# Logits from 64-row matmuls, two sets to a pair of PSUM banks, in a four-layer decoder kernel

## The chip, the core and the metric

The kernel runs on one core of a Trainium2 chip. Five engines work side by side: PE (TensorE, matmuls, with PEld for its weight loads), DVE (VectorE), ACT (ScalarE), POOL (GpSimd) and SP, which issues the DMAs. Each engine takes its own instructions in order and waits on semaphores for the others. The metric is the device time of one execution in microseconds (us), the median of three runs; a trace of one more execution shows every instruction with its start and its duration.

## What is computed

A decoder trunk of four layers over 256 positions, width 1024, all in fp32. A layer projects x to queries, keys and values, mixes tokens, adds attention into 256 memory tokens, projects back, normalises, and runs a SwiGLU feed-forward net (FFN). Layers 0 and 3 use the first of three token mixers, layer 1 the second, layer 2 the third; every mixer has 12 heads of width 64, and the memory attention has 4.

```python
for i in range(DEPTH):
    kind, j = i % N_MIXERS, i // N_MIXERS
    if kind == 0:   # indexer scores choose 64 keys per query, then attention over these
        dots = jnp.einsum('bqhd,bsd->bqhs', qi, k_idx)
        score = jnp.einsum('bqhs,bqh->bqs', jax.nn.relu(dots), wi)   # 8 heads of width 64
        ...
        logits = jnp.einsum('bqhd,bqkhd->bhqk', qb, ks) * scale
        p = jax.nn.softmax(logits, axis=-1)
        ...
    mixed = jnp.concatenate([mix, mo], -1) @ w_out[i]     # mo: memory attention
    x = layer_norm(ALPHA * x + mixed, ln1_g[i], ln1_b[i])
    x = layer_norm(ALPHA * x + swiglu(x, w_gate_up[i], w_down[i]), ln2_g[i], ln2_b[i])
```

## The kernel before

Positions are taken in two blocks of 128 (`tb` 0 and 1). To come near fp32 accuracy, every operand is split into a high part, rounded to fp32r, and a low part, the rest: the high part is a cast on ACT, the low part a subtraction on DVE (`split`, L260), and a product is three matmuls, high by high, high by low and low by high (`mm3`, L253). Weights come in pieces by DMA, ACT casts them (L214), and DVE (L230) or POOL (L228) takes the difference. Projections are L256 to L258.

The order of the work on PE is written out by the program: `K` runs the pieces of a plan one after the other, and between pieces it calls `tick`, which moves a list of small tasks (generators) one step on. A task gives a `yield n` to wait n ticks; so rope, transposes, logits, softmax and the product with the values of a head pair lie between the projection pieces of later ones. On the other engines a scheduler sets the order from priorities.

PSUM has eight banks of 512 fp32 columns. Before, these are eight tiles in a list (`Slots`), taken from the front and put back at the end. A task that finds none free waits a tick.

A *set* of logits belongs to one pair of heads and one `tb`: 128 queries against `nk` = 128 keys (`tb` 0) or 256 (`tb` 1, and the memory attention), for both heads, in one bank. The head width is 64, half the rows of the array. The kernel before fills all 128 rows by stacking: the query tile `q` of a head holds its high part in its own 64 rows and its low part in the other 64 (`q_parts`, L479, one cast and one difference of 64 rows for each head), and the key tile holds the high part of the head in both halves, the low part beside it. For this ACT copies the keys' parts across the halves (`k_cross`, L490, two copies, L492 and L493). One product of 256 keys is then two matmuls for each head (L504, four in a set), one of 128 keys is one for each head, with the high and the low keys side by side (L500, two in a set). There are 80 sets: 24 for the heads and the memory attention in layer 0 and as many in layer 3, counting 8 of the indexer in each, and 16 each in layers 1 and 2.

After a set, `exps` (L515) takes the least of each row on DVE (with a mask L524 and L526, without one L521) and ACT takes the exponential of one head at a time with the row's sum (L529, an ACTIVATE and a READ_ACCUMULATOR each), in place. Three ticks later DVE multiplies by the reciprocal of the sum into `E` or `e` (L542), and the bank goes back. In layers 0 and 3 the indexer's sets are read by a copy and a relu on ACT (L717, L719) and summed on DVE (L728, L730).

Of the kernel before, what the change touches and what calls it, by code (L numbers as in the profile page):

```python
# [84 lines left out]

class Slots:
# [26 lines left out]
class K:  # L113
    def __init__(self, tc, io, ctx):
# [11 lines left out]
        self.banks = Slots([self.pp.tile([128, 512], F32, name=f"bank{i}") for i in range(8)])  # L126
# [10 lines left out]
        self.kks = one([128, 2, 2, S], "k", NKB, F32R)  # L137
# [3 lines left out]
        self.mk = [T([128, 2, 2, S], F32R, f"mk{i}") for i in range(2)]  # L141
# [337 lines left out]
    def q_parts(self, dst, src, scale=None):  # L479

        lo, hi = slice(0, 64), slice(64, 128)
        return [(dst[lo, 0], dst[hi, 0], src[lo], scale), (dst[hi, 1], dst[lo, 1], src[hi], scale)]

    def k_parts(self, dst, src):

        d = dst.rearrange("p h a t -> p a h t")
        n = src.shape[1]
        return d[:, 0], d[:, 1], src[:, None, :].to_broadcast([128, 2, n]), None

    def k_cross(self, dst):  # L490
        lo, hi = slice(0, 64), slice(64, 128)
        self.nc.scalar.copy(dst[hi, 0], dst[lo, 0])  # L492
        self.nc.scalar.copy(dst[lo, 1], dst[hi, 1])  # L493

    def logits(self, b, q, ks, nk):

        mm = self.nc.tensor.matmul
        for h in range(2):
            if nk == 128:
                mm(b[:, h * 256:h * 256 + 256].rearrange("p (a s) -> p a s", a=2), lhsT=q[:, h], rhs=ks[h][:, :, 0:128],  # L500
                   start=True, stop=True)
            else:
                for part in range(2):
                    mm(b[:, h * 256:h * 256 + 256], lhsT=q[:, h], rhs=ks[h][:, part], start=part == 0, stop=part == 1)  # L504

    def pair_logits(self, b, q, kb, nk):
        self.logits(b, q, [kb[:, h] for h in range(2)], nk)

    def read_logits(self, b, nk):
        if nk == 128:  # L510
            L = b.rearrange("p (h a s) -> p h a s", h=2, a=2)
            return L[:, :, 0], L[:, :, 1]
        return (b.rearrange("p (h s) -> p h s", h=2),)
# [17 lines left out]
    def softmax(self, nk, product, mask=None):  # L531

        nc = self.nc
        b = yield from self.tk(self.banks)
        st = yield from self.tk(self.sts)
        e = yield from self.tk(self.es[nk])
        product(b)
        L = self.read_logits(b, nk)
        self.exps(L, e, st[:, 0:2], st[:, 2:4], mask)
        yield W_EXP  # L540
        nc.vector.reciprocal(st[:, 4:6], st[:, 2:4])
        nc.vector.tensor_tensor(e, L[0], st[:, 4:6, None].to_broadcast([128, 2, nk]), op=OP.mult)  # L542
        self.banks.put(b)
        self.sts.put(st)
        yield W_NORM
        return e
# [35 lines left out]
    def qk_task(self, bank, tb, kb, q, flags):  # L582
        b, p = yield from self.rotated(bank, tb)
        q[tb] = yield from self.tk(self.qs)
        k = kb[:, :, :, tb * 128:tb * 128 + 128]
        self.split(self.k_parts(k, p[:, 1]), *self.q_parts(q[tb], p[:, 0], SCALE))
        self.k_cross(k)
        self.banks.put(b)
        yield W_K
        flags.add(("k", tb))  # L590

    def head_task(self, bank, tb, kb, q, flags, masks, vs, vi, col, mix, kbi):
        yield from self.qk_task(bank, tb, kb, q, flags)
        while not (("k", 0) in flags and masks[tb] is not None):
            yield 1
        nk = 128 * (tb + 1)

        def product(b):
            self.pair_logits(b, q[tb], kb, nk)
# [25 lines left out]
    def mk_piece(self, l):  # L625
        b, p = self.t_mode(self.memT, ("mk", l, 0))
        self.split(*(self.k_parts(self.mk[pp], p[:, pp]) for pp in range(2)))
        for pp in range(2):
            self.k_cross(self.mk[pp])
# [10 lines left out]
    def qm_piece(self, l):  # L640
        b, p = self.t_mode(self.xT, ("qm", l, 0))
        qm = [self.take(self.qms, "qm") for _ in range(2)]
        self.split(*(x for pp in range(2) for x in self.q_parts(qm[pp], p[:, pp], SCALE)))
# [4 lines left out]
    def mem_task(self, qm, pp, tb, mix):  # L648
        ts = slice(tb * 128, tb * 128 + 128)

        def product(b):
            self.pair_logits(b, qm[pp][:, :, ts], self.mk[pp], S)
# [12 lines left out]
    def ki_task(self, bank, tb, kb, wi, kg, kbb, flags):  # L665
# [21 lines left out]
        self.split((kb[:, 0, 0, tb * 128:tb * 128 + 128], kb[:, 0, 1, tb * 128:tb * 128 + 128], b[:, 0:128], None))  # L687
# [4 lines left out]
    def qi_task(self, bank, tb, c, qi, mix):  # L692
# [3 lines left out]
        self.split(*(x for i in range(2) for x in self.q_parts(qi[tb, 2 * c + i], p[:, i])))  # L696
# [4 lines left out]
    def select_task(self, tb, qi, kb, wi, flags, masks):  # L701
# [6 lines left out]
        for pr in range(4):  # L708
            while (tb, "ready", pr // 2) not in qi:
                yield 1  # L710
            b = yield from self.tk(self.banks)
            rl = yield from self.tk(self.es[nk])
            self.logits(b, qi[tb, pr], [kb[:, 0]] * 2, nk)
# [151 lines left out]
    def dil_task(self, bank, tb, kb, q, flags, g, parts, jp):  # L865
# [8 lines left out]
        b = yield from self.tk(self.banks)  # L874
        e = yield from self.tk(self.es[nk])
        self.pair_logits(b, q[tb], kb, nk)
# [324 lines left out]
```

## Time and profile before

| | |
|---|---|
| median of 3 runs | 1350.88 us (1350.25 to 1352.53) |
| the profiled execution | 1351.82 us, of which the span of its instructions 1350.0 us |
| mean granted TensorE clock | 0.983 of full speed |
| PE busy | 1287.3 us (95%) |
| DVE / ACT / POOL busy | 897.5 (66%) / 762.9 (57%) / 316.4 us (23%) |

Busy is the union of an engine's instructions in time, so PE's matmuls, which overlap each other, count once. A mean over the span mixes two kinds of stretches: four FFNs with the projections around them, and four mixers. Times within the trace are counted from the start of the span.

### The profile page before, as it was taken

To read this page: it belongs to the slowest core of one execution; us is meant where nothing else is said; L and a number is where in the kernel's file an instruction comes from. 1 tells how busy PE (TensorE), PEld (TensorE's weight loads), DVE (VectorE), ACT (ScalarE), POOL (GpSimd) and SP (SyncE) were. 2 spreads that over 40 slices of the span, in tenths; PEclk is the share of its full clock that TensorE was granted. 3 is DMA by queue.
4 is the path that set the end of the run, shared out by engine and by line. 5 is a ranking of instruction groups with operands and counts; after the bars stand their busy time and mean duration, and the time that the engine had idled before them with its cause. 6 is when DMAs were issued, how large, how long until landed. Compare 5 with 4: busy or idle time off the path is not lost. (4 is left out here: it accounts for less than half of the span.)

```text
span 1350.0 us, 24249 instructions
## 1 busy us (share of the span) xinstructions
PE 1287.3 (95%) x9186; PEld 1212.5 (90%) x9186; DVE 897.5 (66%) x1940; ACT 762.9 (57%) x1512; POOL 316.4 (23%) x277
## 2 busy tenths in 40 slices
PE   6889899999999789999999999999999899999997
PEld 5879799999999779999989989999999898899996
DVE  7887775555578886555567877555568997655555
ACT  5668754444469745444447986444445897544441
POOL 3434440000045343000034444000014533300000
PEclk9989999999999889999999999999999999999999
DMA  8443356556564136565545345666546333655551
GB/s 300 126 149 110 110 180 199 187 188 184 170 203 150 70 103 240 185 189 180 183 155 180 133 141 169 206 185 188 186 138 218 127 125 126 203 188 188 187 176 59
DMA packets 63190, 225.65 MB, mean 167 GB/s; under 512 B 7776, under 2 KB 7776, under 8 KB 63072
## 3 DMA queue, kind: packets, MB, share of 16 engines
q1 hardware_dynamic: 62784, 224.10, 50.2%
q8 instruction: 72, 1.18, 0.4%
q14 instruction: 46, 0.38, 0.1%
q10 hardware_dynamic: 288, 0.00, 0.0%
HBM read 223.02 MB, written 1.05 MB: 166 GB/s over the span
## 5 line engine op out<-in xcount | busy, mean ns | idle before, releaser
L214 ACT CAST wh<-raw 128x1024 fp32r<-128x1024 f32 (+1 forms) x402 | 420.8, 1048 | 318.6 <-PE bank L257 177.2
L230 DVE TENSOR_TENSOR wl<-raw,wh 128x1024 fp32r<-128x1024 f32 (+1 forms) x294 | 378.2, 1288 | 273.9 <-ACT wh L214 269.1
L228 POOL TENSOR_TENSOR wl<-raw,wh 128x512 fp32r<-128x512 f32 x216 | 296.7, 1399 | 727.7 <-ACT wh L214 718.2
L256 PE MATMUL bank<-xh,wh 128*128 128x256 f32 x1344 | 382.1, 284 | 0.0
L257 PE MATMUL bank<-xl,wh 128*128 128x256 f32 x1344 | 381.2, 284 | 0.0
L258 PE MATMUL bank<-xh,wl 128*128 128x256 f32 x1344 | 381.2, 284 | 0.0
L257 PEld LDWEIGHTS bank<-xl,wh 128*128 128x128 f32 x1344 | 258.6, 192 | 1.2
L256 PEld LDWEIGHTS bank<-xh,wh 128*128 128x128 f32 x1344 | 258.6, 192 | 1.3
L258 PEld LDWEIGHTS bank<-xh,wl 128*128 128x128 f32 x1344 | 258.5, 192 | 0.0
L256 PE MATMUL bank<-wh,xh 128*128 128x256 f32 (+1 forms) x768 | 228.5, 298 | 2.8 <-ACT wh L214 1.9
L257 PE MATMUL bank<-wl,xh 128*128 128x256 f32 (+1 forms) x768 | 221.6, 289 | 2.5 <-DVE wl L230 2.3
L258 PE MATMUL bank<-wh,xl 128*128 128x256 f32 (+1 forms) x768 | 221.7, 289 | 0.8 <-DVE xl L270 0.6
L256 PE MATMUL bank<-wh,fth 128*128 128x512 f32 x480 | 189.8, 395 | 0.4 <-ACT fth L265 0.4
L257 PE MATMUL bank<-wl,fth 128*128 128x512 f32 x480 | 188.2, 392 | 0.0
L258 PE MATMUL bank<-wh,ftl 128*128 128x512 f32 x480 | 188.0, 392 | 0.0
L256 PEld LDWEIGHTS bank<-wh,xh 128*128 128x128 f32 x768 | 150.1, 196 | 4.0 <-ACT wh L214 2.4
L257 PEld LDWEIGHTS bank<-wl,xh 128*128 128x128 f32 x768 | 150.1, 195 | 3.1 <-DVE wl L230 3.1
L258 PEld LDWEIGHTS bank<-wh,xl 128*128 128x128 f32 x768 | 149.9, 195 | 1.7 <-DVE xl L270 1.7
L258 PEld LDWEIGHTS bank<-wh,ftl 128*128 128x128 f32 x480 | 90.5, 189 | 19.9 <-DVE ftl L270 0.7
L256 PEld LDWEIGHTS bank<-wh,fth 128*128 128x128 f32 x480 | 90.7, 189 | 17.5 <-ACT fth L265 0.8
L257 PEld LDWEIGHTS bank<-wl,fth 128*128 128x128 f32 x480 | 90.7, 189 | 16.3
L1061 ACT CAST fth<-sil 128x256 fp32r<-128x256 f32 x80 | 32.5, 406 | 107.3 <-DVE sil L1059 107.3
(194 smaller groups left out, 1553.0 us busy)
## 6 DMA issues: line engine op xcount, KB each, us to landing
raw<-in_w SPq DMA_DIRECT2D x396, 512.0 KB, 3.9
lng<-in_ln_g SPq DMA_DIRECT2D x8, 512.0 KB, 4.0
lnb<-in_ln_b SPq DMA_DIRECT2D x8, 512.0 KB, 6.2
raw<-in_w SPq DMA_DIRECT2D x4, 492.0 KB, 4.8
x<-in_xT SPq DMA_DIRECT2D x2, 512.0 KB, 5.4
E<-in_mem SPq DMA_DIRECT2D x4, 256.0 KB, 5.6
x<-in_x SPq DMA_DIRECT2D x2, 512.0 KB, 6.0
out_x<-x SPq DMA_DIRECT2D x4, 256.0 KB, 2.2
```

Source lines behind the costliest of these rows:

```text
L214: self.nc.scalar.copy(c[0][:, 0:wd], self.raw[n][:, 0:wd])
L228: self.nc.gpsimd.tensor_tensor(lo[:, c], r[:, c], hi[:, c], op=OP.subtract)
L230: self.nc.vector.tensor_tensor(lo[:, 0:wd], r[:, 0:wd], hi[:, 0:wd], op=OP.subtract)
L256: mm(out, lhsT=ah, rhs=bh, start=first, stop=False)
L257: mm(out, lhsT=ah, rhs=bl, start=False, stop=False)
L258: mm(out, lhsT=al, rhs=bh, start=False, stop=last)
L1061: nc.scalar.copy(fts[i][0], s)
```

## The change

The two heads of a pair are no longer stacked. `q` and `k` hold the high and the low part of both heads, each head in its own 64 rows (`parts_of`), so one cast and one difference of 128 rows make either, and `k_cross` goes. A set's logits are matmuls of 64 rows, the first head on rows 0 to 63, the second on rows 64 to 127, in turn, each head into a bank of its own: six for 256 keys (three for each head), four for 128 keys (two of 256 columns, two of 128). A set takes 256 columns of two neighbouring banks (`pop2`): the first set that asks opens a pair of free banks and takes one half of the columns, the next takes the other half, and a pair goes back to the list when both halves are free. `pop` takes the bank that has been free longest, and prefers one whose neighbour is taken. The bank is asked for after `st` and `e`. All banks are one tile, `bank`.

The core of the diff; the memory keys (`mk_piece`), their queries (`qm_piece`), the indexer (`ki_task`, `qi_task`, `select_task`) and `dil_task` change in the same way:

```diff
+class Banks:
+    def __init__(self, tile):
+        self.tile, self.now = tile, 0
+        self.free = {i: i - 8 for i in range(8)}
+        self.halves = {}
+
+    def pop(self):
+        i = min(self.free, key=lambda i: self.free[i] + (4 if i ^ 1 in self.free else 0))
+        del self.free[i]
+        return self.tile[:, i]
+
+    def pop2(self):
+        if not self.halves:
+            ps = [i for i in self.free if not i % 2 and i + 1 in self.free]
+            if not ps:
+                return None
+            i = min(ps, key=lambda i: max(self.free[i], self.free[i + 1]))
+            t = max(self.free.pop(i), self.free.pop(i + 1))
+            self.halves = {(i, 0): t, (i, 1): t}
+        i, c = min(self.halves, key=self.halves.get)
+        del self.halves[i, c]
+        return self.tile[:, i:i + 2, c * 256:c * 256 + 256]
+
+    def put(self, x):
+        self.now += 1
+        first, col = x.offset % 4096 // 512, x.offset % 512
+        if len(x.shape) == 2:
+            self.free[first] = self.now
+            return
+        c = col // 256
+        self.halves[first, c] = self.now
+        if (first, 1 - c) in self.halves:
+            for d in range(2):
+                del self.halves[first, d]
+                self.free[first + d] = self.now
...
-        self.banks = Slots([self.pp.tile([128, 512], F32, name=f"bank{i}") for i in range(8)])
+        self.banks = Banks(self.pp.tile([128, 8, 512], F32, name="bank"))
...
-        self.kks = one([128, 2, 2, S], "k", NKB, F32R)
+        self.kks = one([128, 2, S], "k", NKB, F32R)
...
-        self.mk = [T([128, 2, 2, S], F32R, f"mk{i}") for i in range(2)]
+        self.mk = [T([128, 2, S], F32R, f"mk{i}") for i in range(2)]
...
-    def q_parts(self, dst, src, scale=None):
-        lo, hi = slice(0, 64), slice(64, 128)
-        return [(dst[lo, 0], dst[hi, 0], src[lo], scale), (dst[hi, 1], dst[lo, 1], src[hi], scale)]
-    def k_parts(self, dst, src):
...
-    def k_cross(self, dst):
-        lo, hi = slice(0, 64), slice(64, 128)
-        self.nc.scalar.copy(dst[hi, 0], dst[lo, 0])
-        self.nc.scalar.copy(dst[lo, 1], dst[hi, 1])
...
+    def parts_of(self, dst, src, scale=None):
+        return dst[:, 0], dst[:, 1], src, scale
+
+    def tk2(self):
+        while (b := self.banks.pop2()) is None:
+            yield 1
+        return b
+
+    def logits(self, bs, q, k, nk):
         mm = self.nc.tensor.matmul
...
+        rows = [slice(0, 64), slice(64, 128)]
         if nk == 128:
+            for h, r in enumerate(rows):
+                mm(bs[:, h, 0:256].rearrange("p (a s) -> p a s", a=2), lhsT=q[r, 0], rhs=k[r, :, 0:128], start=True, stop=False)
+            for h, r in enumerate(rows):
+                mm(bs[:, h, 0:128], lhsT=q[r, 1], rhs=k[r, 0, 0:128], start=False, stop=True)
+            return
+        for n, (a, c) in enumerate(((0, 0), (0, 1), (1, 0))):
+            for h, r in enumerate(rows):
+                mm(bs[:, h, 0:256], lhsT=q[r, a], rhs=k[r, c], start=n == 0, stop=n == 2)
+
+    def read_logits(self, bs, nk):
+        return [bs[:, :, c:c + nk] for c in range(0, 256, nk)]
...
     def softmax(self, nk, product, mask=None):
         nc = self.nc
-        b = yield from self.tk(self.banks)
         st = yield from self.tk(self.sts)
         e = yield from self.tk(self.es[nk])
+        b = yield from self.tk2()
...
-        self.split(self.k_parts(k, p[:, 1]), *self.q_parts(q[tb], p[:, 0], SCALE))
-        self.k_cross(k)
+        self.split(self.parts_of(k, p[:, 1]), self.parts_of(q[tb], p[:, 0], SCALE))
```

The sequence of pieces on PE is the same before and after: with the matmuls of a set counted as one, the two lists are equal, piece by piece. Three places show what differs. In the orders, "[waits ...]" names the engines whose semaphores an instruction waits for, and a name ends in the number of its buffer.

PE, layer 0, the indexer: `fth_124` and `ftl_121` in the kernel before, `fth_117` and `ftl_114` in the changed one, are query tiles, `k` the indexer's keys, the `wh` and `xh` rows are projections. First before, then the change:

```order
L258 MATMUL bank_68<-wh_75,xl 128x256
L500 MATMUL bank_69<-k_135,fth_124 128x256 [waits DVE_49]
L500 MATMUL bank_69<-k_135,fth_124 128x256 [waits DVE_49,Activation_49]
L504 MATMUL bank_64<-k_135,ftl_121 128x256 x4
L256 MATMUL bank_65<-xh,wh_77 128x256 [waits DVE_49]
```

```order
L297 MATMUL bank<-wh_68,xl 128x256
L533 MATMUL bank<-k_128,fth_117 128x256 [waits DVE_49]
L533 MATMUL bank<-k_128,fth_117 128x256
L535 MATMUL bank<-k_128,fth_117 128x128 x2
L539 MATMUL bank<-k_128,ftl_114 128x256 [waits Activation_49]
L539 MATMUL bank<-k_128,ftl_114 128x256 x5
L295 MATMUL bank<-xh,wh_70 128x256
```

The two sets stand next to each other in both; before they write banks of their own (69 and 64), now they write the two halves of banks 0 and 1, and the second waits for ACT (the relu of the first, by the number that it waits for).

PE, layer 3, the heads: `q_92` of the kernel before and `q_85` of the changed one belong to a set of 256 keys, `q_91` and `q_84` to one of 128; `ident,e` is a transpose.

```order
L555 MATMUL bank_63<-ident,e_97 128x128
L504 MATMUL bank_66<-k_137,q_92 128x256 x4
L500 MATMUL bank_68<-k_135,q_91 128x256 [waits Activation_49] x2
L256 MATMUL bank_65<-wh_75,xh 128x256
L257 MATMUL bank_65<-wl_76,xh 128x256
```

```order
L585 MATMUL bank<-ident,e_90 128x128
L539 MATMUL bank<-k_130,q_85 128x256 [waits Activation_49] x2
L539 MATMUL bank<-k_130,q_85 128x256 x4
L533 MATMUL bank<-k_128,q_84 128x256 [waits DVE_49]
L533 MATMUL bank<-k_128,q_84 128x256 [waits Activation_49]
L535 MATMUL bank<-k_128,q_84 128x128 x2
L295 MATMUL bank<-wh_68,xh 128x256
```

Here the second set takes the first columns of banks 6 and 7 and the first set the last 256. The waits of the L533 rows name DVE (the normalisation of the set that had these columns) and ACT (the second exponential of the set that stands just ahead, in the other columns).

ACT, layer 0, between the first two sets of the memory attention and the first heads: `q`, `k`, `nat`, `pah` and `fth` as in the code, `st` the row values of an exponential.

```order
L265 CAST k_137<-bank_65 128x2x128
L267 ACTIVATE q_90<-bank_65 64x128 x2
L529 ACTIVATE bank_66,st_147<-bank_66,st_147 128x256 x2
L465 COPY nat_89<-bank_64 128x256
L492 COPY k_137<-k_137 64x2x128
L529 ACTIVATE bank_67,st_148<-bank_67,st_148 128x128
L493 COPY k_137<-k_137 64x2x128
L529 ACTIVATE bank_67,st_148<-bank_67,st_148 128x128
```

```order
L559 ACTIVATE bank,st_141<-bank,st_141 128x128 x2
L304 CAST pah_95<-bank 128x256
L304 CAST k_130<-bank 128x128
L306 ACTIVATE q_83<-bank 128x128
L504 COPY nat_82<-bank 128x256
L253 CAST wh_70<-raw_67 128x1024
L304 CAST fth_113<-bank 64x128 x2
L304 CAST pbh_99<-bank 128x512
```

The two copies across the halves and one of the two casts of `q` are gone; the exponentials stand between the same kinds of neighbours.

## Rows read from the trace of the kernel before

**Rows 1.** Page, part 1: busy time, share, instructions of each engine.

```profile
PE 1287.3 (95%) x9186; PEld 1212.5 (90%) x9186; DVE 897.5 (66%) x1940; ACT 762.9 (57%) x1512; POOL 316.4 (23%) x277
```

**Rows 2.** Busy time by stretch: start:end, length, engines (instructions), granted clock, DMA.

```profile
core 0: us, PE busy (x) PEld busy (x) DVE busy (x) ACT busy (x) POOL busy (x), PEclk, DMA share, GB/s
34.00:178.00 144.00, 128.51 (x911) 121.71 (x910) 114.27 (x359) 101.97 (x259) 62.50 (x54) 0.94 0.36 123
178.00:371.00 193.00, 193.00 (x1383) 182.82 (x1382) 107.57 (x135) 91.36 (x127) 17.84 (x14) 1.00 0.59 189
371.00:506.00 135.00, 121.85 (x856) 114.35 (x855) 109.45 (x291) 89.48 (x223) 61.23 (x45) 0.94 0.39 131
700.00:822.00 122.00, 116.91 (x872) 110.09 (x872) 95.76 (x275) 91.20 (x233) 57.31 (x44) 1.00 0.45 150
1005.00:1165.00 160.00, 151.47 (x1114) 142.31 (x1114) 140.29 (x430) 117.56 (x289) 69.23 (x59) 1.00 0.43 146
```

**Rows 3.** Waits of PE: line, releaser, us in total, times, longest us.

```profile
PE bank L555 <- DVE E L913: 4.9, 2, 4.0
PE bank L504 <- ACT k L492: 2.3, 3, 0.9
PE bank L500 <- ACT k L492: 2.0, 1, 2.0
```

**Rows 4.** Groups by line: count, busy us, mean ns, idle before.

```profile
L504 PE MATMUL bank<-k,q 128*128 128x256 f32 x96 | 17.9, 307 | 4.8 <-ACT E L529 2.5 <-ACT k L492 2.3
L500 PE MATMUL bank<-k,q 128*128 128x256 f32 x48 | 11.1, 308 | 2.2 <-ACT k L492 2.0
L492 ACT CAST k<-k 64x256 fp32r<-64x256 f32 x48 | 19.4, 404 | 6.5 <-DVE k L270 5.2
L267 ACT ACTIVATE q<-bank 64x128 fp32r<-64x128 f32 x96 | 26.0, 271 | 0.6
L272 DVE SCALAR_TENSOR_TENSOR q<-bank,q 64x128 fp32r<-64x128 f32 x96 | 27.7, 288 | 2.5
```

**Rows 5.** Timeline, PE then ACT, at 80 and 1133: start, us, what.

```profile
79.93 0.72 PE L504 MATMUL bank<-k,q 128*128 128x256 f32 x4
80.97 0.20 ACT L529 ACTIVATION_READ_ACCUMULATOR bank<-bank,st 128x1 f32 x1
...
1133.52 0.64 PE L504 MATMUL bank<-k,q 128*128 128x256 f32 x4
1133.95 0.20 ACT L529 ACTIVATION_READ_ACCUMULATOR bank<-bank,st 128x1 f32 x1
```

**Rows 6.** Timeline at 108.7 to 111.6, PE and ACT: start, us, what.

```profile
108.74 0.64 PE L504 MATMUL bank<-mk,qm 128*128 128x256 f32 x4
109.22 0.28 PE L256 MATMUL bank<-wh,xh 128*128 128x256 f32 x1
...
111.27 0.36 PE L256 MATMUL bank<-wh,xh 128*128 128x256 f32 x1
111.30 0.19 ACT L529 ACTIVATION_READ_ACCUMULATOR bank<-bank,st 128x1 f32 x1
111.47 0.28 PE L257 MATMUL bank<-wl,xh 128*128 128x256 f32 x1
```

**Rows 7.** Timeline at 1073.8 to 1079.4, PE then ACT.

```profile
1073.80 0.72 PE L504 MATMUL bank<-k,q 128*128 128x256 f32 x4
1074.36 0.40 PE L500 MATMUL bank<-k,q 128*128 128x256 f32 x2
...
1079.20 0.19 ACT L529 ACTIVATION_READ_ACCUMULATOR bank<-bank,st 128x1 f32 x1
```

**Rows 8.** Timeline at 40.4 to 42.3, PE then ACT.

```profile
40.43 0.40 PE L500 MATMUL bank<-k,fth 128*128 128x256 f32 x2
40.67 0.64 PE L504 MATMUL bank<-k,ftl 128*128 128x256 f32 x4
...
41.85 0.38 ACT L717 COPY e<-bank 128x256 f32<-128x256 f32 x1
```

More of the change, by code (lines that the diff above doesn't have):

```diff
@@ L475, in rotated @@
         return b, p
-    def q_parts(self, dst, src, scale=None):
-        lo, hi = slice(0, 64), slice(64, 128)
-        return [(dst[lo, 0], dst[hi, 0], src[lo], scale), (dst[hi, 1], dst[lo, 1], src[hi], scale)]
-    def k_parts(self, dst, src):
-        d = dst.rearrange("p h a t -> p a h t")
-        n = src.shape[1]
-        return d[:, 0], d[:, 1], src[:, None, :].to_broadcast([128, 2, n]), None
-    def k_cross(self, dst):
-        lo, hi = slice(0, 64), slice(64, 128)
-        self.nc.scalar.copy(dst[hi, 0], dst[lo, 0])
-        self.nc.scalar.copy(dst[lo, 1], dst[hi, 1])
@@ L495, in logits @@
-    def logits(self, b, q, ks, nk):
-        mm = self.nc.tensor.matmul
[L498 to L507, printed above, removed]
@@ L584, in qk_task @@
         q[tb] = yield from self.tk(self.qs)
-        k = kb[:, :, :, tb * 128:tb * 128 + 128]
-        self.split(self.k_parts(k, p[:, 1]), *self.q_parts(q[tb], p[:, 0], SCALE))
-        self.k_cross(k)
+        k = kb[:, :, tb * 128:tb * 128 + 128]
+        self.split(self.parts_of(k, p[:, 1]), self.parts_of(q[tb], p[:, 0], SCALE))
         self.banks.put(b)
@@ L598, in product @@
         def product(b):
-            self.pair_logits(b, q[tb], kb, nk)
+            self.logits(b, q[tb], kb, nk)
             self.qs.put(q[tb])
@@ L626, in mk_piece @@
         b, p = self.t_mode(self.memT, ("mk", l, 0))
-        self.split(*(self.k_parts(self.mk[pp], p[:, pp]) for pp in range(2)))
-        for pp in range(2):
-            self.k_cross(self.mk[pp])
+        self.split(*(self.parts_of(self.mk[pp], p[:, pp]) for pp in range(2)))
         self.banks.put(b)
@@ L642, in qm_piece @@
         qm = [self.take(self.qms, "qm") for _ in range(2)]
-        self.split(*(x for pp in range(2) for x in self.q_parts(qm[pp], p[:, pp], SCALE)))
+        self.split(*(self.parts_of(qm[pp], p[:, pp], SCALE) for pp in range(2)))
         self.banks.put(b)
@@ L651, in product @@
         def product(b):
-            self.pair_logits(b, qm[pp][:, :, ts], self.mk[pp], S)
+            self.logits(b, qm[pp][:, :, ts], self.mk[pp], S)
         e = yield from self.softmax(S, product)
@@ L686, in ki_task @@
         nc.tensor.transpose(b[:, 0:128], kd, self.ident)
-        self.split((kb[:, 0, 0, tb * 128:tb * 128 + 128], kb[:, 0, 1, tb * 128:tb * 128 + 128], b[:, 0:128], None))
+        self.split(self.parts_of(kb[:, :, tb * 128:tb * 128 + 128], b[:, 0:128]))
         self.banks.put(b)
@@ L695, in qi_task @@
             qi[tb, 2 * c + i] = mix[2 + 2 * c + i][tb].rearrange("p (h t) -> p h t", h=2)
-        self.split(*(x for i in range(2) for x in self.q_parts(qi[tb, 2 * c + i], p[:, i])))
+        self.split(*(self.parts_of(qi[tb, 2 * c + i], p[:, i]) for i in range(2)))
         self.banks.put(b)
@@ L710, in select_task @@
                 yield 1
-            b = yield from self.tk(self.banks)
             rl = yield from self.tk(self.es[nk])
-            self.logits(b, qi[tb, pr], [kb[:, 0]] * 2, nk)
+            b = yield from self.tk2()
+            self.logits(b, qi[tb, pr], kb, nk)
             L = self.read_logits(b, nk)
@@ L873, in dil_task @@
         st = parts[jp, tb, "st"]
-        b = yield from self.tk(self.banks)
         e = yield from self.tk(self.es[nk])
-        self.pair_logits(b, q[tb], kb, nk)
+        b = yield from self.tk2()
+        self.logits(b, q[tb], kb, nk)
         self.qs.put(q[tb])
```

4 lines of the change are left out of this document (removed).

## The prediction

> **What bounds the kernel now.** Read first the busy times of the whole page, then the same by stretch. PE is busy for 1287.3 us of 1350 [rows 1], and by stretch this splits in two: in an FFN PE has no gap at all (193.00 of 193.00 us), in the four mixers it has them: 128.51 of 144, 121.85 of 135, 116.91 of 122 and 151.47 of 160 us, 518.7 of 561 together, so 42.3 us idle [rows 2]. No engine but PE is full there: DVE has 459.8 and ACT 400.2 of the 561 us. So PE's own order sets the time, and in the mixers it is broken by waits for results that come late out of the queues of DVE and ACT. The listed waits say of whom: mostly of DVE, with the combination of the dilated groups the largest (4.9 us in two waits), of ACT's copies of the keys across the halves only 2.3 and 2.0 us [rows 3]. The granted clock tells a second price of gaps: in the two mixers with 15.5 and 13.2 us of idle it is 0.94 in the mean, in the two with 5.1 and 8.5 us it is 1.00 [rows 2]. A stretch at 0.94 of 144 us has lost 8.6 us of PE's work, one of 135 us 8.1.
>
> The FFNs hold none of the changed steps. All that follows is in the 561 us of mixers, and every us that PE waits more or works less there counts in full, since PE's order of pieces stays.
>
> **What goes from ACT and DVE.** A head's task loses two copies of 404 ns on ACT (48 of L492 [rows 4], as many of L493: 38.8 us), and half of 96 casts of q of 271 ns (13.0 us); the same for the memory and the indexer, by their sizes, makes some 76 us in all, a fifth of ACT's 400. DVE loses half of 96 steps of 288 ns [rows 4], 13.8 us, and with the rest some 30 of 460. Neither engine bounds a mixer, so this is worth only what PE waited for it. The 4.3 us behind the copies [rows 3] go; next late is the low part of k and q on DVE, which stands ahead of the copies today. From DVE's waits a fifteenth, its share of work removed, may go too, 2 us of the 32 that are left when 4.3 and some 6 of other ACT waits are taken from 42.3. That is -6. Bounds: 0, if something else comes late at the same places, and -16, if all ACT waits and a fifth of the rest go.
>
> **The logits themselves.** A matmul of 256 columns leaves PE free after 0.12 us: four of them start at 108.74 and the next starts at 109.22 [rows 6]. Before, there are 192 of L504 and 64 of L500 (two more groups of 64 and 32, and one of 16, beside the rows shown [rows 4]): 256 x 0.12 = 30.7 us. After, 48 sets have six and 32 have four (two of them of 128 columns, which I put at 0.11, close to the 0.12 of a longer one, since no row shows one here). If the two heads, on different rows of the array, run at the same time: 48 x 3 x 0.12 + 32 x (0.12 + 0.11) = 24.6 us, 6 less. If one after the other: 49.3 us, 18.6 more. No row shows a matmul of 64 rows. I take +2, a third of the way from the better end, because weight loads already lie under other matmuls (1212.5 us of them under 1287.3 [rows 1]), so the machine overlaps such steps.
>
> **Changing between 128 and 64 rows.** The 80 sets form 75 runs, so PE changes its form 150 times. At a change the pipeline may run on or empty. The nearest row is the step from transposes to a projection: the projection's first matmul at 111.27 holds PE until 111.47, 0.20 us in place of 0.12 [rows 6], 0.08 lost. Bounds: nothing, and what a matmul lasts beyond its slot, 0.28 - 0.12 = 0.16 us: 150 times 0 to 0.16 is 0 to 24.5 us. I take 0.08, 12 us.
>
> The Trainium skill, "TensorEngine Tiling (Array Packing)", section "Tiling Modes", speaks against the change here: changing the tiling mode, not just the tile, drains the TensorE. By that rule the upper bound, 24.5 us, would stand in the sum in place of 12. No run here shows it yet.
>
> **The waits that the change adds.** The two sets of a pair lie in the same banks, and the build makes the second wait until the readers of the first are done, though the columns differ: of the 80 sets, 34 wait so, 33 of them for exponentials. PE stops at the first matmul of the second set, and all projections queue behind it; ACT and DVE do not stop. How long is read from the set before: from its first matmul to the end of its second exponential the 33 pairs take 5.8 us in the mean today (shortest of all sets 2.75: 108.74 to 111.49 [rows 6]), while the second set follows after 0.6 to 11 us. Laid over today's trace, PE would reach the second set too early in 30 of the 33 pairs, the first by 81.17 - 79.93 = 1.24 us, the last by 1134.15 - 1133.52 = 0.63 us [rows 5], the longest in layer 3, where two sets stand back to back: 1079.39 - 1074.36 = 5.03 us [rows 7]. The 30 sum to 59.5 us. The indexer of layer 0 adds its own: two sets at 40.43 and 40.67, where the first's copy ends at 42.23 [rows 8] and an add and a relu follow; the second must now wait for these, over 2 us, and so a second time: 4.5 us. The ceiling is 64 us. The floor takes the 2.75 us for every pair: 10 us, with the indexer 14.5. I take 22, nearer to the floor: ACT has a fifth less to do, so its queue ahead of the exponentials is shorter; while PE stands, ACT and DVE catch up, so that the next pair waits less; and part of it falls where PE waited anyway. The long end is not excluded, because half of what comes before an exponential is DVE's, and DVE stays at 430 of 561 us.
>
> **Clock.** 22 us more of gaps bring the two quiet mixers from 5.1 and 8.5 us to where the others are now, and those had 8.1 and 8.6 us of lost clock. Between 0 and 17; I take 6.
>
> **How the numbers follow.** The profiled execution took 1351.82 us, 0.94 over the median. The sum: -6 + 2 + 12 + 22 + 6 = +36 us. That is 1387.8 for such an execution, 1387 for the median. A difference of 0.2% (2.7 us) is about what a measurement of this kernel can tell from none.
>
> **The rivals.** *Faster, because ACT's relief shortens the way from a set to its exponentials.* Its place is ACT's queue ahead of the exponentials, its price all of the 22 us and more, and it decides once the 5.8 us fall to about 3: then only the back-to-back pairs wait, some 12 us, partly in idle time, the 14 us behind late operands go, heads run at the same time (-6) and changes cost nothing: 1350.9 - 14 - 6 + 12 = 1343. For it: 76 us fewer on ACT. Against it: the masks and minima on DVE stand in that way too. The Trainium skill, "TensorE: Matmul & The Clock Gate", Part 3 on packing, says that matmuls on different row groups run concurrently, four of them 3.07 times as fast as one after the other; by that the logits would stand at the end of -6. Chance 0.17.
>
> *Much slower: 64-row matmuls run one after the other and every change of form empties the pipeline.* +18.6 + 24.5 + 22 + 8 - 6 = +67: 1418. Against it only that nothing in the array asks for it. Chance 0.20.
>
> *No difference: the new waits fall into the idle time that DVE makes anyway.* PE's 42.3 us of idle are larger than the 22. With -6 and -6 against 12 for the changes: 1351. Against it: the two quiet mixers have only 5.1 and 8.5 us of idle, and hold 21 of the 33 pairs. Chance 0.08.
>
> That the change does not do what it says, and pairs are never shared, is excluded by the order. The forecast has 0.55, and its own range is 1362 to 1408. The range for 8 in 10 reaches to half of either outer rival: 1342 to 1420. Faster: 0.17 and 0.02 of the third rival, 0.19; same 0.05; slower 0.55 + 0.20 + 0.01 = 0.76.
>
> **What would show it.** The FFN stretches should keep their length to 1 us. Each mixer should be longer, the idle of PE should rise from 42 to some 65 us, and among PE's waits the lines of the new logits should appear with the exponentials on ACT as the releaser, 34 or fewer times, 1 us each or so, some 4 and 5 us. The copies' line is gone, ACT is some 76 us less busy, DVE 30. The start of a second head's matmul right behind the first's (some ns) or 0.12 us later tells which end of the logits holds, and the first start behind a set tells the cost of a change. The clock in layers 2 and 3 tells the last term. The forecast is wrong if the way from a set to its exponentials falls below 3.5 us, or if the waits of PE stay as few as they are.

## The result: 1385.0 us, 2.4% slower, and where it went

The changed kernel takes 1385.03 us in the median of 4 runs (1382.25 to 1388.73); the kernel before took 1351.7 on the same chip. The ratio is 1.024 (1.021 to 1.028). The forecast was 1387 us. Its total was right, but in good part by luck: two large errors in its terms cancel, and the experiments below say which. The trace is of the slowest of the four runs, 1388.73 us, at a mean granted clock of 0.970 (up to 0.977 in the others), so the clock's share is likely smaller in the median run than in the rows below.

The changed code moves the lines by 39: the projections L256 to L258 are now L295 to L297, the transposes of q and k (L473) are L512, those of the softmax's result (L555) are L585, and the logits stand in L533 and L535 (128 keys) and L539 (256 keys). The busy times of the whole page, against [rows 1]:

```profile
PE 1321.7 (95%) x9346; PEld 1227.9 (89%) x9346; DVE 860.5 (62%) x1868; ACT 688.2 (50%) x1328; POOL 317.7 (23%) x277
```

The relief came in full: ACT is some 75 us less busy, DVE 37. PE is busier by 34.4. The same by stretch, laid over the same work as [rows 2] (four mixers, and the first FFN as second row; the columns are start:end, length, busy time of each engine, granted clock, DMA):

```profile
34.00:184.00 150.00, 133.16 (x961) 121.98 (x961) 104.02 (x340) 82.23 (x213) 60.73 (x53) 0.93 0.37 123
184.00:377.00 193.00, 193.00 (x1382) 182.81 (x1381) 106.78 (x136) 88.75 (x123) 18.48 (x14) 1.00 0.60 189
377.00:507.00 130.00, 124.78 (x878) 113.88 (x878) 96.28 (x277) 74.14 (x185) 61.19 (x46) 0.95 0.40 134
702.00:830.00 128.00, 122.74 (x904) 112.77 (x903) 88.45 (x259) 77.57 (x195) 58.70 (x45) 0.97 0.42 141
1012.00:1201.00 189.00, 169.84 (x1164) 153.27 (x1163) 134.99 (x406) 100.19 (x243) 68.78 (x58) 0.93 0.37 125
```

The FFN keeps its 193.00 us. The mixers take 597 us in place of 561, and some 28 of the 36 us lie in layer 3. PE's idle time in them is 16.8 + 5.2 + 5.3 + 19.2 = 46.5 us, 4.2 more than before; its busy time is 31.8 more. Of that the clock explains some 17.3: length times what is missing to 1.00 was 16.7 us before (8.6 and 8.1, in layers 0 and 1) and is 10.5 + 6.5 + 3.8 + 13.2 = 34.0 now. Layer 3, whose clock was 1.00, alone lost 13.2 us. This is an estimate: the rows give the clock to two places, and the length counts idle time too (with busy time in its place the difference is 16.1). The remaining 14.5 us of busy time are put down to the 64-row logits.

What PE waits for (line, tile, releaser, us in total, times, longest):

```profile
PE bank L512 <- DVE bank L497: 6.4, 1, 6.4
PE bank L539 <- ACT bank L559: 5.7, 3, 3.2
PE bank L539 <- DVE E L572: 5.3, 4, 1.8
PE bank L512 <- DVE pal L309: 3.8, 1, 3.8
PE bank L512 <- DVE nat L499: 3.4, 1, 3.4
PE bank L533 <- DVE E L572: 3.3, 1, 3.3
PE bank L512 <- DVE ftl L309: 3.2, 4, 1.0
...
PE bank L512 <- DVE k L309: 2.3, 1, 2.3
PE bank L539 <- ACT bank L746: 2.2, 1, 2.2
PE bank L539 <- DVE sil L755: 2.0, 1, 2.0
PE bank L512 <- DVE pbl L309: 1.9, 2, 1.4
...
PE bank L533 <- ACT bank L559: 1.5, 1, 1.5
...
PE bank L512 <- DVE kd L708: 0.4, 1, 0.4
```

In the kernel before, the same two places have these rows beside those of the copies in [rows 3]:

```profile
PE bank L473 <- DVE kd L681: 7.0, 2, 6.2
PE bank L473 <- DVE nat L460: 5.9, 5, 2.6
...
PE bank L504 <- ACT E L529: 2.5, 1, 2.5
```

Two things are to be seen. The logits' lines wait 20.0 us in 11 waits for exponentials (L559), normalisations (L572) and the indexer's steps; before it was 6.8. And L512, the transposes of q and k, waits 21.4 us (12.9 before, none of it for a split), of which 3.8, 3.2, 2.3 and 1.9 us are for splits (L309) that have nothing to do with what is transposed. The likely reading is that they are the last readers of the bank that L512 is to write. That is a shortage of banks, which the prediction did not have.

### The profile page after: what moved, and what is told of

Its sections match the earlier page's. It is cut to its first block, busy times and chain, and to the rows that moved or that the text cites. A ratio compares the mean times of both kernels' runs of the same rounds, so it can differ in the third digit from the quotient of the medians.

```text
span 1387.0 us, 24327 instructions
## 1 busy us (share of the span) xinstructions
PE 1321.7 (95%) x9346; PEld 1227.9 (89%) x9346; DVE 860.5 (62%) x1868; ACT 688.2 (50%) x1328; POOL 317.7 (23%) x277
## 4 chain that ended last, share of the span: by engine, by line
PE 82%; DVE 9%; ACT 5%; issue 2%; DMA 1%; POOL 1%; SPq 0%; DVEq 0%; ACTq 0%; POOLq 0%
PE bank L295 26%; PE bank L297 25%; PE bank L296 25%; ACT wh L253 2%; PE bank L539 1%; DVE wl L269 1%; DMA raw<-in_w 1%; PE bank L585 1%; ACT bank L559 1%; PE bank L512 1%; DVE ftl L309 1%; PE bank L361 1%; POOL wl L267 1%; DVE bank L556 1%; DVE E L572 0%
## 5 line engine op out<-in xcount | busy, mean ns | idle before, releaser
L295 PE MATMUL bank<-xh,wh 128*128 128x256 f32 x1344 | 382.4, 285 | 0.0
L297 PE MATMUL bank<-xh,wl 128*128 128x256 f32 x1344 | 380.9, 283 | 0.0
L295 PEld LDWEIGHTS bank<-xh,wh 128*128 128x128 f32 x1344 | 258.1, 192 | 2.2 <-issue 0.2
L297 PEld LDWEIGHTS bank<-xh,wl 128*128 128x128 f32 x1344 | 258.3, 192 | 0.0
L295 PE MATMUL bank<-wh,xh 128*128 128x256 f32 (+1 forms) x768 | 238.6, 311 | 1.8 <-ACT xh L304 0.9
L296 PE MATMUL bank<-wl,xh 128*128 128x256 f32 (+1 forms) x768 | 226.8, 295 | 1.8 <-DVE wl L269 1.7
L297 PE MATMUL bank<-wh,xl 128*128 128x256 f32 (+1 forms) x768 | 226.7, 295 | 0.9 <-DVE xl L309 0.7
L295 PE MATMUL bank<-wh,fth 128*128 128x512 f32 x480 | 191.1, 398 | 0.4 <-ACT fth L304 0.4
L297 PE MATMUL bank<-wh,ftl 128*128 128x512 f32 x480 | 188.0, 392 | 0.0
L295 PEld LDWEIGHTS bank<-wh,xh 128*128 128x128 f32 x768 | 155.2, 202 | 7.5 <-ACT xh L304 1.5
L296 PEld LDWEIGHTS bank<-wl,xh 128*128 128x128 f32 x768 | 155.5, 202 | 2.7 <-DVE wl L269 2.7
L297 PEld LDWEIGHTS bank<-wh,xl 128*128 128x128 f32 x768 | 154.9, 202 | 1.7 <-DVE xl L309 1.7
L297 PEld LDWEIGHTS bank<-wh,ftl 128*128 128x128 f32 x480 | 90.6, 189 | 20.2 <-DVE ftl L309 0.7
L295 PEld LDWEIGHTS bank<-wh,fth 128*128 128x128 f32 x480 | 90.9, 189 | 18.7 <-ACT fth L304 0.8
```

The costliest lines, as they stand in the source:

```text
L295: mm(out, lhsT=ah, rhs=bh, start=first, stop=False)
L296: mm(out, lhsT=ah, rhs=bl, start=False, stop=False)
L297: mm(out, lhsT=al, rhs=bh, start=False, stop=last)
```

## The experiments

The base beside each run is the kernel before on the same chip, 1352.8 to 1354.1 us. In the diffs "-" is the kernel named.

**The relief alone.** The kernel before with the operands of the change, but 128-row matmuls (so that the two heads are summed) and the eight separate banks.

```diff
-        self.split(self.k_parts(k, p[:, 1]), *self.q_parts(q[tb], p[:, 0], SCALE))
-        self.k_cross(k)
+        self.split(self.parts_of(k, p[:, 1]), self.parts_of(q[tb], p[:, 0], SCALE))
...
-                    mm(b[:, h * 256:h * 256 + 256], lhsT=q[:, h], rhs=ks[h][:, part], start=part == 0, stop=part == 1)
+                    mm(o, lhsT=q[:, part], rhs=k[:, part], start=part == 0, stop=part == 1)
```

> The kernel before with the changed operands alone: q and k hold the high and the low part of both heads in 128 rows, made by one cast and one difference each, and the copies across the halves are gone. A set of logits keeps its own bank of the eight and its four or two matmuls of 128 rows, as before; so each product here runs over both heads' rows at once and the heads are not kept apart: that part of the computation is changed, its time is not. What differs from the kernel before is the work on ACT and DVE, 76 and 30 us less. The theory of the prediction (PE waits little for these engines): 6 us less than before, 1345, at most 16 less. The rival that ACT's relief shortens everything: 20 us less or more.

1323.55 us, 0.978 (0.976 to 0.979): 29.7 us faster, where the prediction had 6 and at most 16; the rival's 20 or more holds. The mixers by stretch:

```profile
34.00:164.00 130.00, 122.47 (x911) 117.71 (x911) 101.78 (x340) 81.90 (x213) 60.22 (x52) 0.95 0.42 141
...
357.00:485.00 128.00, 119.09 (x852) 112.29 (x851) 101.48 (x278) 73.89 (x186) 60.37 (x46) 0.96 0.40 136
679.00:794.00 115.00, 114.58 (x869) 109.39 (x868) 87.56 (x258) 76.66 (x195) 58.13 (x45) 1.00 0.46 155
977.00:1136.00 159.00, 153.10 (x1112) 144.72 (x1111) 132.07 (x406) 99.41 (x243) 71.04 (x58) 0.98 0.44 149
```

PE's idle time fell from 42.3 to 22.8 us, in layer 0 most of all. That is 19.5 of the 29.7 us; PE's busy time in the mixers fell too, from 518.7 to 509.2, with the same matmuls. No run splits this second part.

**The pairs with 128-row matmuls.** The changed kernel, all its banks and its sharing, with the matmuls of the run above.

```diff
-                mm(bs[:, h, 0:256], lhsT=q[r, a], rhs=k[r, c], start=n == 0, stop=n == 2)
+                    mm(bs[:, h, 0:256], lhsT=q[:, part], rhs=k[:, part], start=part == 0, stop=part == 1)
```

> The changed kernel with matmuls of 128 rows in place of 64, four or two of 256 columns in a set, written into the same halves of the same pairs of banks (heads not kept apart, as in r1). PE has no change of form any more. In the trace of the changed kernel a set of 256 keys holds PE 0.98 us from the projection ahead to the second projection behind, 0.26 more than before, one of 128 keys 0.81, 0.33 more: 48 x 0.26 + 32 x 0.33 = 23 us. The theory that the change of form is the largest part: 23 us less than the changed kernel, 1362. The theory that the waits for the other half of the bank hold most: 1375 or more, with PE's waits at the logits as in the changed kernel (some 25 us).

1371.16 us, 1.013 (1.010 to 1.015), between the two theories: the 64-row form is worth 13.9 us and not 23, and the rest is with the banks. So the banks, their sharing and the rule for them cost 47.6 us over the relief alone. The four mixers here, as in the changed kernel above:

```profile
33.00:180.00 147.00, 127.58 (x911) 121.44 (x911) 102.68 (x339) 82.35 (x213) 60.51 (x52) 0.93 0.37 127
...
373.00:504.00 131.00, 122.72 (x854) 114.68 (x853) 99.30 (x279) 75.20 (x186) 62.15 (x46) 0.95 0.39 133
698.00:822.00 124.00, 118.45 (x873) 112.86 (x872) 87.65 (x259) 77.50 (x195) 59.01 (x45) 0.97 0.43 146
1004.00:1186.00 182.00, 159.87 (x1108) 149.01 (x1108) 133.48 (x406) 99.95 (x241) 68.67 (x58) 0.95 0.38 130
```

The logits (L532, L535) and the transposes (L512) wait, as in the changed kernel:

```profile
PE bank L535 <- ACT bank L555: 5.6, 5, 2.4
PE bank L512 <- DVE bank L497: 5.3, 1, 5.3
PE bank L535 <- DVE E L568: 4.8, 4, 1.9
PE bank L512 <- DVE nat L499: 4.1, 2, 3.5
PE bank L512 <- DVE ftl L309: 3.5, 4, 1.0
PE bank L532 <- DVE E L568: 3.4, 1, 3.4
```

All waits at the logits sum to 27.0 us (1.4 in the run of the relief), those at L512 to 20.7 (10.4).

**No sharing.** The changed kernel, with a set alone in a pair of banks, and a second form that shares only when no pair is free.

```diff
-        if not self.halves:
...
-        i, c = min(self.halves, key=self.halves.get)
-        del self.halves[i, c]
-        return self.tile[:, i:i + 2, c * 256:c * 256 + 256]
+        ps = [i for i in self.free if not i % 2 and i + 1 in self.free]
...
+        del self.free[i], self.free[i + 1]
+        return self.tile[:, i:i + 2, 0:256]
```

> The changed kernel with a pair of banks taken by one set alone, the second half of its columns unused. No set waits for the readers of another in the same banks. The theory of the prediction: the 20 us or so that PE waits ahead of its logits go, 1365 to 1370. The rival: two whole banks taken by every set leave too few for the transposes and the projections, whose waits for a bank's last reader (in the changed kernel's trace some 15 us already, against 2 before) grow by as much or more: 1385 or slower.

> The changed kernel, but a set opens a new pair of banks while one is free, and takes the second half of an open one only when none is. Sets share less often, and banks are short less often than with no sharing at all. The theory of shared banks: between the changed kernel and the one without sharing, 1370 to 1380. The rival (banks are short): the same as the changed kernel or slower, 1385 to 1395.

1414.27 us, 1.046 (1.043 to 1.048), and 1413.45 us, 1.044 (1.043 to 1.046): 29 us slower than with sharing. The rival holds in the first; the second is above both of its ranges and no faster than the first. In the first of the two the longest waits are now at the transposes (L577 and L504 here), for splits that read the bank last:

```profile
PE bank L577 <- DVE ftl L301: 18.5, 12, 2.6
PE bank L504 <- DVE ftl L301: 7.6, 8, 1.4
PE bank L504 <- DVE pbl L301: 5.0, 4, 2.0
```

Sharing is not the worse of two evils: without it the banks run out.

**Two banks fewer, and the rule.** Both on the kernel of the relief alone, with no pairs: six separate banks; and eight with the change's rule for the next bank (and its one tile for all banks).

```diff
-        self.banks = Slots([self.pp.tile([128, 512], F32, name=f"bank{i}") for i in range(8)])
+        self.banks = Slots([self.pp.tile([128, 512], F32, name=f"bank{i}") for i in range(6)])
```

```diff
-        self.banks = Slots([self.pp.tile([128, 512], F32, name=f"bank{i}") for i in range(8)])
+        self.banks = Banks(self.pp.tile([128, 8, 512], F32, name="bank"))
```

> The kernel of r1 (operands of the change, 128-row matmuls, each set alone in one of separate banks; the two heads' logits are summed, so it leaves out their separation) with six banks in place of eight. r1 took 1323.6 us, r2, with the shared pairs, 1371.2: 47.6 us more. Theory 'shortage': most of the 47.6 is PE (transposes and projections) waiting for a bank's last reader, because sets hold pairs; two banks fewer then cost a good part of it with no sharing at all: 1343 to 1375, and the waits at the transposes' line grow. Theory 'sharing': most of it is the second set of a pair waiting for the readers of the first; six separate banks then stay within some 8 us of r1: 1323 to 1332.

> The kernel of r1 with the changed kernel's rule for the next bank (free longest first, a bank whose neighbour is taken preferred) and its single tile of eight banks, but no pairs: each set is alone in one bank. Theory of the pairs: the rule costs nothing by itself, 1320 to 1327. Rival: the rule, which spares whole pairs, hands single banks out too early; then part of the 47.6 us between r1 and r2 shows here, 1330 or more.

Six banks: 1378.24 us, 1.018 (1.017 to 1.020), 54.7 over the relief, some 7 of them in and behind the FFNs. The waits at the transposes of q and k grow from 10.4 to 19.2 us, as the theory "shortage" has it; the time is a little above its range. Two banks are worth as much as all that the pairs cost. The rule: 1334.79 us, 0.986 (0.984 to 0.988), 11.2 over the relief, so it isn't free, and the rival holds. It prefers a bank whose neighbour is taken over one that has been free longer. That leaves 36.4 us between the rule and the run with pairs, which also asks for its bank later, after `st` and `e`; no run tells these two apart.

**The waits of sharing alone.** A matmul of 4 columns ahead of every second set, written into the bank of the set before it, so that it waits for that set's readers; the eight banks stay as they were. Once on the kernel of the relief, once on the kernel before.

```diff
         mm = self.nc.tensor.matmul
+        old = self.open
+        if old is None or old[1] != self.banks.uses.get(id(old[0])):
+            self.open = b, self.banks.uses[id(b)]
+        else:
+            mm(old[0][:, 0:4], lhsT=q[:, 0], rhs=k[:, 0, 0:4], start=True, stop=True)
+            self.open = None
```

> The kernel of r1 (eight separate banks, each set alone in one, 128-row matmuls, heads summed) with a matmul of 4 columns ahead of every second set, written into the bank of the set before it if that bank has not been taken anew: 39 of them. Each has to wait for the readers of that set as the second set of a pair does, but no bank is held longer and none is spared; it spoils 4 columns of the earlier set's logits. The matmuls themselves are worth some 3 us. Between r6 and r2 lie 36.4 us for the pairs. Theory 'sharing' (the prediction's 22, and its clock): 20 to 40 us over r1, 1344 to 1364. Theory 'shortage' (r5: two banks fewer cost 54.7 us): the waits are small or fall where PE waits anyway, 3 to 12 us, 1326 to 1336.

> The kernel before with the same 39 matmuls of 4 columns as in r11, each written into the bank of the set before it, so that it waits for that set's readers; it spoils 4 columns of the earlier set's logits. Operands, copies and banks stay as before. Theory 'separate prices': the waits cost as much as on top of r1 (50.9 us), and the relief is worth 29.7 us with or without them: 1398 to 1410. Theory 'one answers the other': without the waits ACT and DVE run behind PE without being waited for at the sets, with them the relief is on the way at every second set and is worth more: 1411 or more. Theory of the prediction: waits 22 us and clock 6, relief 6 us beside them: 1377 to 1390.

With the relief 1374.46 us, 1.015 (1.014 to 1.017), above the range of either theory, on the side of "sharing". Without it 1411.57 us, 1.043 (1.041 to 1.044), on the border of the first two theories, which it does not tell apart; the third is out. The waits cost 50.9 us on the one and 57.5 on the other, and the relief is worth 37 us in their presence, 29.7 without. PE's waits at the added matmul, without the relief (all of this line):

```profile
PE bank L506 <- ACT bank L539: 28.8, 19, 3.9
PE bank L506 <- DVE sil L740: 13.9, 6, 4.9
PE bank L506 <- ACT e L539: 11.0, 2, 9.5
...
PE bank L506 <- DVE e L552: 4.3, 1, 4.3
PE bank L506 <- ACT bank L729: 4.3, 2, 2.4
...
PE bank L506 <- ACT E L539: 2.1, 1, 2.1
```

They sum to 64.4 us in 31 waits; with the relief to 42.1 in 25. The prediction's overlay of the trace of before, 30 waits of 59.5 us and 4.5 for the indexer, was 64. But the waits are not what the 57.5 us consist of: by the same stretches as above PE's idle time in the mixers grows by 37.0 us only (42.3 to 79.3), since PE waits less at other lines, and its busy time by 20.0, which the clock can account for (39.2 us lost in place of 16.7).

**ACT's copies alone.** The kernel before without the two copies across the halves.

```diff
-        self.k_cross(k)
...
-        for pp in range(2):
-            self.k_cross(self.mk[pp])
```

> The kernel before without the two copies of the keys across the halves (ACT, 48 times 2 of 404 ns and 8 times 2 of 617 ns, 48.7 us; it leaves out that each half gets the other head's keys). It is the part of the relief that falls on ACT alone; DVE's work stays. r1, with ACT 75 us and DVE 37 us less busy, gained 29.7 us. Theory 'ACT': the copies stand in ACT's queue ahead of the exponentials and gain in proportion, 48.7/75 of 29.7, some 19 us: 1330 to 1340. Theory 'DVE': DVE's shorter steps made the gain; then only the some 4 us of the waits that the profile puts on the copies go: 1347 to 1352.

1335.55 us, 0.987 (0.986 to 0.989): 17.3 us for 48.7 us of ACT's work, as the theory "ACT" has it. PE's waits that name the copies sum to 4.3 us [rows 3], a quarter of it. The other 12 us of the relief (casts of q, DVE's steps) have no run of their own.

**The change of form by itself.** One more matmul of 256 columns in 80 places of the FFNs, with 128 and with 64 rows.

```diff
                 cs = slice((k % 4) * 256 + c * 128, (k % 4) * 256 + c * 128 + 128)
+                if key[0] == "gu" and k == 0 and c == 0:
+                    self.nc.tensor.matmul(p[:, c], lhsT=w[0][0:64, cs], rhs=xT[0][0:64, 0], start=True, stop=True)
```

> The kernel before with one more matmul of 128 rows and 256 columns in 80 places of the FFNs (4 layers, 20 each), where PE has no gap; its product is written over by the next matmul, so nothing of the result is left out. Both theories: 80 times 0.12 = +9.6 us, 1362 to 1364. It is the base for r10.

> As r9, but the matmul has 64 rows, so that PE changes its form 160 times where nothing else makes it wait. Theory of the prediction: a change costs 0.08 us, 12.8 us more than r9, 1374 to 1378. Rival, from the slots around the sets in the trace of the changed kernel (a set of 256 keys took 0.26 us more, one of 128 keys 0.33, two changes each): 0.13 to 0.19 a change, 21 to 30 us more than r9, 1383 to 1395.

1363.44 us (1.008, 1.006 to 1.009) and 1394.90 us (1.030, 1.029 to 1.032). The 128-row matmuls cost 10.5 us, 0.13 each. The 64-row ones cost 31.5 more: 160 changes of 0.197 us. The same place in the two traces (start, duration, line; L299 is the added one), first with 128 rows, then with 64:

```profile
218.35 0.28 PE L258 MATMUL bank<-xh,wl 128*128 128x256 f32 x1
218.47 0.28 PE L299 MATMUL bank<-xh,wh 128*128 128x256 f32 x1
218.59 0.28 PE L256 MATMUL bank<-xh,wh 128*128 128x256 f32 x1
218.71 0.28 PE L257 MATMUL bank<-xl,wh 128*128 128x256 f32 x1
```

```profile
218.54 0.28 PE L258 MATMUL bank<-xh,wl 128*128 128x256 f32 x1
218.75 0.38 PE L299 MATMUL bank<-xh,wh 64*128 64x256 f32 x1
219.06 0.38 PE L256 MATMUL bank<-xh,wh 128*128 128x256 f32 x1
219.28 0.28 PE L257 MATMUL bank<-xl,wh 128*128 128x256 f32 x1
```

Steps of 0.12 us become 0.21 into the 64-row matmul, 0.31 out of it and 0.22 for the one behind: 0.74 in place of 0.36, so 0.19 for each change. What is called a change here holds all that a lone 64-row matmul costs beyond one of 128 rows.

**A version faster than both.** The kernel before with its result whole and its eight banks: each head of q and k is written twice ahead of the transposes, and the splits then write whole tiles, with no copies across the halves.

```diff
-        self.nc.scalar.copy(n, bank[:, 0:256])
+        nc.scalar.copy(n4, bank[:, 0:256].rearrange("p (h d) -> p h d", h=4)[:, :, None, :].to_broadcast([128, 4, dup, 64]))
...
-        self.split(self.k_parts(k, p[:, 1]), *self.q_parts(q[tb], p[:, 0], SCALE))
-        self.k_cross(k)
+        nc.scalar.copy(d[:, 0], p[:, 2:4])
+        nc.scalar.activation(q[tb], p[:, 0:2], AF.Copy, scale=SCALE)
+        nc.vector.tensor_tensor(d[:, 1], p[:, 2:4], d[:, 0], op=OP.subtract)
+        nc.vector.scalar_tensor_tensor(q[tb][hi], p[hi, 0:2], SCALE, q[tb][hi], op0=OP.mult, op1=OP.subtract)
```

> The kernel before, all of its result kept, with each head of q and k written twice into the buffer ahead of the transposes (ACT's copy of 256 columns becomes one of 512), four transposes in place of two, and then whole splits: no copies across the halves, q's two half casts become one, k's stays. Buffers for it: 2 in place of 3 of twice the size, 8 small ones in place of 12. Worked out: PE 48 times 2 more transposes of 0.11 = +10.5 us; ACT a task 2.13 us before, some 1.4 after, -35 us in all; DVE about even. Theory 'ACT': -35/75 of 29.7 = -14, with +10.5 some -3: 1345 to 1353. Theory 'DVE': nothing gained but the 4 us at the copies, 1356 to 1364.

1339.77 us, 0.990 (0.988 to 0.992): 13 us faster than the kernel before, and better than either theory had it.

```profile
PE 1287.6 (96%) x9282; PEld 1216.2 (91%) x9282; DVE 890.3 (67%) x1892; ACT 725.7 (54%) x1368; POOL 315.3 (24%) x277
```

PE does 96 transposes more in the same busy time as before (1287.3, [rows 1]); the granted clock is 0.989 in place of 0.983. ACT fell by 37 us.

## The prediction, step by step

The length of each mixer, from the same matmul to the same matmul in every trace (us; worked out from the starts on PE):

| kernel | layer 0 | layer 1 | layer 2 | layer 3 | median |
|---|---|---|---|---|---|
| before | 144.0 | 134.9 | 122.0 | 160.1 | 1352.8 |
| relief alone | 129.9 | 127.7 | 115.2 | 158.7 | 1323.6 |
| relief and rule | 133.6 | 126.1 | 117.2 | 164.9 | 1334.8 |
| relief, rule and pairs | 147.0 | 130.3 | 123.8 | 181.9 | 1371.2 |
| changed kernel | 149.5 | 130.5 | 128.1 | 188.1 | 1385.0 |
| relief and waits | 145.3 | 136.9 | 123.7 | 177.6 | 1374.5 |
| before and waits | 158.9 | 144.3 | 130.3 | 186.1 | 1411.6 |

**The relief, -6 with bounds of 0 and -16: wrong.** It is -29.7 alone and -37 where the waits of sharing are there. The prediction also took 4.9 us at the dilated groups for the largest of the listed waits; that is one row, and the largest is the 7.0 us at L473 shown above. The step that failed is the pricing of a busy engine by the waits that name it. The list of waits names the last releaser only; an engine's queue delays everything behind it. The copies show it: 4.3 us by the list, 17.3 by the run without them. What they delay can be seen in the way from a set's first matmul to the end of its second exponential: 6.0 us in the mean of all 64 such sets before, 5.5 without the copies, 4.6 with the relief.

**The waits of sharing, 22 of a possible 64: near the changed kernel's own list, wrong as a price.** The changed kernel waits 20.0 us at its logits, 11 times and not 30. But as a price on the kernel before, the sharing costs 57.5 us, 37.0 of it in gaps and some 20 in clock, where the prediction had 22 and 6. The reason given for the low end, that ACT's relief shortens its queue, is worth little: with the relief the waits at the added matmul fall from 64.4 to 42.1 us, but their price only from 57.5 to 50.9.

**How the total came out right.** The measured differences in a row are -29.7 for the relief, +47.6 for the banks (rule, sharing and holding, with the clock that they cost) and +13.9 for the 64-row form, 31.8 together. The prediction's terms for them are -6, 22 + 6, and 2 + 12, together 36. The gain was too small by 23.7 us and the price of the banks by 19.6; that the two errors cancel is luck.

**The shortage of banks: missed.** The prediction had no term for a pair that is held until both of its sets have been read, nor for the rule. The rule costs 11.2 us. Six banks without any pair cost 54.7 us, and sets alone in whole pairs 29 us more than the change. How the 36.4 us of the pairs split between sharing and holding stays open: each costs more than that by itself (50.9 and 54.7), so they don't add. The waits at the sets themselves get fewer as the kernel has more else to wait for (42.1 us in the run of the waits alone, 27.0 with the pairs, 20.0 in the changed kernel). It may be that PE, held for a bank at L512, comes later to the next set and waits less there; no run shows it.

**The logits and the change of form, +14: right in sum, by two errors.** The run against 128 rows gives 13.9, the estimate from the busy time 14.5. Two heads do run at the same time: of 208 second heads 185 start within 10 ns of the first, 3 ns in the median. A set of six in the changed kernel, against the four at 108.74 in [rows 6]:

```profile
110.08 0.28 PE L297 MATMUL bank<-wh,xl 128*128 128x256 f32 x1
110.28 0.62 PE L539 MATMUL bank<-mk,qm 64*128 64x256 f32 x6
110.84 0.39 PE L295 MATMUL bank<-wh,xh 128*128 128x256 f32 x1
111.06 0.28 PE L296 MATMUL bank<-wl,xh 128*128 128x256 f32 x1
```

So the logits were at their better end, 6 us less, and the change of form above the upper bound of 0.16: 0.19 to 0.20, 150 times, some 29 us if each counted in full. They don't all: against the run with 128 rows the changed kernel's mixers have 21.9 us more busy time (550.5 and 528.6), of which some 4 are clock (34.0 us lost in place of 29.7), and 8.9 us less idle time (46.5 and 55.4). The likely reason is that a change behind a wait falls into time that PE would have waited; no run shows it apart.

By the Trainium skill, "TensorEngine Tiling (Array Packing)", section "Tiling Modes", a change of the tiling mode drains the engine. The trace agrees in that both changes cost time, and their 0.19 us are somewhat more than what a matmul lasts beyond its slot. By the Trainium skill, "TensorE: Matmul & The Clock Gate", Part 3, matmuls on different row groups run concurrently. The 3 ns agree.

**The clock, +6 with a bound of 17: near the bound, some 17 in the profiled run.** It fell where the prediction looked for it, in layers 2 and 3 (1.00 to 0.97 and 0.93). That the idle time rises to 65 us was wrong: it went to 46.5. In the run with the pairs and 128 rows, PE has as many matmuls as the kernel of the relief, 9186, and is busy 1299.7 us in place of 1280.4: these 19 us have no other place than the clock and the modelled ends. The prediction took idle time as the clock's measure, and that doesn't hold here: layer 1 of the changed kernel has 5.2 us of idle and 0.95, where layer 3 of the kernel before has 8.5 and 1.00. What sets it stays open.

**The rivals.** The faster one had its condition met: the way to the exponentials is 3.3 us in the changed kernel, below the 3.5 that the prediction named as what would make the forecast wrong. It did not come all the same, so that sign misled. The relief gave more than its 14 us, but it had 12 for the banks, which cost 47.6, and -6 for the 64-row form, which cost 13.9. The much slower one was half right (every change of form costs more than 0.16 us, but the heads are not serial). The third failed: part of the new waits do fall into idle time, which grew by 4.2 us only, but the busy time grew by 31.8.

## What to carry to other kernels

Price an engine's relief by its queue and not by the waits that name it: take the work out in a run, or follow what stands behind it. Count banks as a resource of their own, with what each allocation holds and until when; here two of eight were worth 55 us, nearly twice all that the lighter operands gained. And check the terms of a forecast one by one with runs, as a right total can stand on two wrong ones.

## What the hardware showed that was not expected

A single 64-row matmul between 128-row ones costs 0.38 us beyond its slot, at both of its ends and in the second step behind it (0.21, 0.31 and 0.22 us in place of 0.12). The same holds at the sets: 0.20 us ahead of the first 64-row matmul at 110.28, and 0.22 from the first 128-row one behind them to the next. And the granted clock of a stretch, a mean over it, does not follow its idle time alone: it was 1.00 with 8.5 us of idle in layer 3 before, and 0.95 with 5.2 in layer 1 of the changed kernel. In one trace each, layer 3 had 0.93 with 19.2 us of idle in the changed kernel and 0.95 with 22.1 in the run with 128 rows.
